# A two-layer encoder trunk: layer 1's modulation computed in the up passes, and no dots in its output projection

## The chip, the cores and the metric

The kernel runs on one core of a Trainium2 chip. The metric is the device time of one execution in microseconds. Matmuls run on TensorE (PE; its weight loads are PEld), elementwise work on VectorE (DVE), ScalarE (ACT) and GpSimd (POOL). All loads and stores are issued by SyncE (SP), whose queue is worked off in order: an issue that has to wait holds those behind it.

## The reference

The sequence has 1024 tokens of width 1024 in float32. Layer 0 mixes with multi-head latent attention, layer 1 with an mLSTM, and each is followed by a gated MLP with a causal convolution over three tokens. What matters here is the modulation: six vectors per layer, each 1024 long, computed from the conditioning vector c.

```python
c_act = jax.nn.silu(c)
for i in range(DEPTH):
    mod = c_act @ mod_w[i] + mod_b[i]
    sh_a, sc_a, g_a, sh_f, sc_f, g_f = [t[:, None, :] for t in jnp.split(mod, 6, axis=-1)]
    h = rms_norm(x) * (1 + sc_a) + sh_a
    y = mixer(h, ...)                      # layer 0: attention, layer 1: mLSTM; ends in @ w_out
    x = x + g_a * y
    h = rms_norm(x) * (1 + sc_f) + sh_f
    x = x + g_f * conv_ffn(h, ...)         # (gelu(conv(h @ w_up_a)) * (h @ w_up_g)) @ w_down
```

Parts 0 to 5 of a layer's modulation are, in this order, shift, scale and gate of the mixer and shift, scale and gate of the MLP.

## The kernel before

The activations lie with the channels on the partitions, as eight tiles of 128 channels by 512 tokens for each half of the sequence (`hf` 0 and 1). Every float32 product is made of three matmuls (`mm3`, L173 to L179), from operands split into a high and a low part. For a weight tile `wraw` or `raw`, ScalarE writes the high part `whi` (L169, L964) and GpSimd or VectorE the low part `wlo` (L170, L965).

A **dot** (`mod_dot`, L201) computes 128 entries of the modulation: a tile `mraw` of 128 rows of `mod_w` by 1024, 512 KB, is loaded (L213), VectorE multiplies it by the row `crow` = silu(c) and sums along the row into a column of `modc`. Eight dots make a part, and `mod_bias` (L206) adds the bias to it. `mod_steps` (L208) is a generator that deals this out: at each step it does the dot whose load was issued a step before, and then issues the next load. Its tiles have two buffers, so a load waits for the dot two before it. Dots are kept in the written order among themselves; everything else is ordered on each engine by the framework's scheduler from the order and the priority in which it is written.

The stages that the change touches are these.

- **Layer 0's MLP, up pass** (`mlp`, L941 on). 154 products of 12 matmuls, `pa`, `pb` and `pd`, numbered i = 0 to 153, with their operands derived by VectorE from `raw` tiles of `in_wf` (four buffers), then convolution (`ct`, L1004 to L1007) and gating (L1011), and a store of each result to memory (`ud`). After product i the function `extra(i)` is called; here it takes one step of layer 1's modulation at every third product from i = 30 on (L1275). Parts 1, 0 and 2 of layer 1, 24 dots, end about product 102.
- **Layer 0's down pass**, in the same sequence: its operands `U` are derived on VectorE from the stored values (`q`), its products `da` and `db` are gated into x (`gate_x`, L299).
- **Layer 1's mixer**, which uses `crow` as scratch; it is loaded and passed through silu again at L1626.
- **Layer 1's output projection** (`out_proj`, L848). For each half and each of the eight channel tiles m: load and split a weight tile (`unit`, L166 to L170), make the product `op` of 24 matmuls, gate it into x (L299), store x (`xd`, L846), square it on ScalarE (`sq`) and add the squares on VectorE (`ssq`, L246). The second half loads all eight weight tiles once more. After the first half, the sixteen small matmuls `st` (L255) sum the squares over the partitions, GpSimd takes the root (L260), and the transposes `rb` (L267) spread it; then x becomes the operands of the up pass. `up_ps` banks and `X_WAIT`, `X_RSTD` say how many products later this is written. Ahead of each m the projection calls `extra(hf, m)`: two steps of layer 1's modulation in the first half, one in the second (L1628 to L1630). These are parts 4 and 3, sixteen dots.
- **Layer 1's up pass**, which takes part 5, eight dots, from product 60 on, and its down pass with the final norm.

Of the kernel before, what the change touches and what calls it, by code (L numbers as in the profile page):

```python
# [11 lines left out]
F32 = mybir.dt.float32  # L12
# [6 lines left out]
P = 128  # L19
D = 1024  # L20
S = 1024
KT = D // P
HS = 512
# [64 lines left out]
U_MQ, U_MK, U_MV, U_MO, U_MG, U_OUT1 = 0, 4, 8, 16, 24, 25  # L88
# [11 lines left out]
def trunk_kernel(ctx: ExitStack, tc: tile.TileContext, xT, pos, c_d, cols_d, mod_w, win, winT, w0, w1, wf, wd, out):  # L100
# [4 lines left out]
    def nm(s):  # L105
        n_names[0] += 1
        return f"{s}_{n_names[0]}"
# [8 lines left out]
    def phase(name, **kw):  # L116
        st = ExitStack()
        p = st.enter_context(tc.tile_pool(name=name, bufs=1, reuse_waits="tile", **kw))
        return st, p
# [11 lines left out]
    def block(i, shape, dt, name):  # L131
        return blk.tile(shape, dt, tag=f"b{i}", name=nm(name))
# [67 lines left out]
    def mod_dot(l, i, raw):  # L200
        return dve.scalar_tensor_tensor(raw, raw, 1.0, crow, ALU.mult, ALU.mult, accum_out=modc[l][:, i:i + 1])  # L201

    def mod_bias(l, i, n=1):

        mc, b = modc[l][:, i:i + n], COL[f"mb{l}"] + i
        dve.scalar_tensor_tensor(mc, mc, 1.0 if i // 8 in (1, 4) else 0.0, cols_at(b, n), ALU.add, ALU.add)  # L206

    def mod_steps(l, parts, raw_tile, stop=None):  # L208

        for j in parts:  # L210
            for k in range(KT):
                raw = raw_tile()
                nc.sync.dma_start(raw, mod_w[l, j * 8 + k])  # L213
                yield
                tc.keep_in_program_order(mod_dot(l, j * 8 + k, raw))
            mod_bias(l, j * 8, KT)
            if j == stop:
                yield
# [100 lines left out]
    xs = [block(0, [P, KT, HS], F32, "x"), None]  # L319
# [437 lines left out]
    mods = mod_steps(0, (2, 4, 3, 5), lambda: mod_raw(), 3)  # L757
# [22 lines left out]
    def piece(gen, n=1):  # L780
        for _ in range(n):
            next(gen, None)
# [16 lines left out]
    for n in range(2 * NH):  # L799
        q, kk, qr, kvu, i, hf, head = args.pop(0)  # L800
# [47 lines left out]
    def out_proj(px, psC, osrc, us, w, l, extra=None, early=0):  # L848

        def up_ps(name):  # L850
            return psC.tile([P, HS], F32, tag="up", bufs=4, name=nm(name))

        stN, pn = phase("pn", side="right")
        xs, T = [], {}
        for hf in range(2):
            o, x = osrc(hf)
            xs.append(x)
            ssq = Squares(pn)
            for m in range(KT):
                if extra is not None:  # L860
                    extra(hf, m)
                if hf or m >= early:
                    ps = op_mm(o, us.pop(0) if us else unit(w[m]))
                    gate_x(x[:, m, :], m, ps, l, 2)
                store_x(2 * l, hf, m, x)
                ssq.keep(x[:, m, :]) if m == KT - 1 else ssq.add(x[:, m, :])
            if hf == 0:
                hh, hl = h_tiles(0)
                T["B11"], T["B21"] = [(hh[:, i:i + 4], hl[:, i:i + 4]) for i in (0, 4)]
                rstd_later(ssq, D, T["B11"], lambda rb: operands_first(xs[0], rb, l, hh, hl), X_WAIT[0],  # L870
                           up_ps, X_RSTD[0])
        for n, i in (("T1", 1), ("B22", 6), ("T2", 5), ("T3", 7)):
            t = (px if i > 5 else blk).tile([P, KT, HS], F32R, tag=f"b{i}", name=nm(n))
            T[n] = t[:, 0:4], t[:, 4:8]
        rstd_later(ssq, D, T["T1"], lambda rb: operands_second(px, xs, rb, l, T), X_WAIT[1], up_ps,
                   X_RSTD[1])
        stN.close()
        return xs, T
# [367 lines left out]
    pF = []  # L1246
# [3 lines left out]
    u_d = [[[dram.tile([P, HS], F32, name=f"ud{l}_{m}_{hf}") for hf in range(2)] for m in range(FT)] for l in range(2)]  # L1250

    stX, px, stP, psC = open_ffn(1)

    def o_src(hf):
        return (whole(o_back(1)), load_res(1, lambda hf, m: xT[m, :, hf * HS:(hf + 1) * HS])) if hf else oA

    stR, pr = phase("pr", side="right")
    mod_raw = lambda: pr.tile([P, D], F32, tag="mraw", bufs=2, name=nm("mraw"))
    xs, T = out_proj(px, psC, o_src, us, [w0[U_OUT0 + m] for m in range(KT)], 0,
                     lambda hf, m: piece(mods, MODS_OUT[hf][m]), EARLY)  # L1260
    for _ in mods:
        pass
    stR.close()
    mods = mod_steps(1, (1, 0, 2), lambda: pF[0].tile([P, D], F32, tag="mraw", bufs=2, name=nm("mraw")))
    hs = []

    def done(hf, t0, w, x, ssq):
# [4 lines left out]
                 W0[hf], W0_RSTD[hf])  # L1272

    pD = []
    mlp(px, psC, T, 0, u_d[0], pD, done, ((0, HS),), lambda i: piece(mods, i >= 30 and i % 3 == 0))  # L1275
    for _ in mods:
        pass
    h = hs
# [341 lines left out]
    stX, px, stP, psC = open_ffn(2)  # L1620

    def y_split(hf):
        return whole(split_o(hf, ys[hf])), load_res(hf, lambda hf, m: x_d[1][hf][m])

    stR, pr = phase("pr", side="right")
    nc.sync.dma_start(crow, c_d.broadcast_to([P, D]))  # L1626
    act.activation(crow, crow, AF.Silu)
    mods = mod_steps(1, (4, 3), lambda: pr.tile([P, D], F32, tag="mraw", bufs=2, name=nm("mraw")))  # L1628
    xs, T = out_proj(px, psC, y_split, [], [w1[U_OUT1 + m] for m in range(KT)], 1,
                     lambda hf, m: piece(mods, 2 if hf == 0 else 1))  # L1630
    for _ in mods:
        pass
    stR.close()
    mods = mod_steps(1, (5,), lambda: pF[0].tile([P, D], F32, tag="mraw", bufs=2, name=nm("mraw")))

    def gain(x, m):
# [14 lines left out]
    pD = []  # L1651
# [102 lines left out]
```

## Time and profile before

| what | value |
|---|---|
| three timed runs | 2292.92, 2294.84, 2308.62 us |
| median of the three | 2294.84 us |
| the profiled execution | 2296.64 us |
| span of its instructions | 2294.6 us |
| mean granted TensorE clock | 0.978 |

The span runs from the first to the last instruction; the 2.0 us by which the time is longer lie outside it. In a row of the timeline stand start, duration, engine, line, operation, what is written and what is read, and in brackets how long the engine was idle just before, with what ended that idle time. A row of a stretch has the busy time and the count of instructions for each engine, the clock that TensorE was granted as a share of its full speed, the mean busy share of the sixteen DMA engines and the rate. Matmuls overlap: one of 512 columns shows about 0.39 us, but starts follow each other by 0.227, so times of the stages are taken from starts.

Layer 0's up pass runs from 506.6 us to about 948, layer 1's output projection from 1519.0 to 1632.8, its up pass from there on.

### The profile page before, as it was taken

What the parts mean: (1) busy time and instruction counts of PE and PEld (TensorE: products, weight loads), DVE (VectorE), ACT (ScalarE), POOL (GpSimd) and SP (SyncE); (2) the same over time, 40 slices, a digit from 0 to 9 for tenths busy, and PEclk for the clock granted to TensorE, in tenths of its full rate; (3) what the DMA queues carried; (4) which work ended last, traced back from release to release, by engine and by line L of the source; (5) the groups of instructions that cost most, each with busy time, mean ns of one, the idle gap of its engine ahead of it and who ended that gap; (6) DMA issues with size and microseconds to landing.
All of it is one profiled execution on the core that took longest, in us unless ns stands there. A gap on an engine that the chain in (4) does not pass through costs nothing. (4 is left out here: it accounts for less than half of the span.)

```text
span 2294.6 us, 28893 instructions
## 1 busy us (share of the span) xinstructions
PE 2199.4 (96%) x10553; PEld 1838.3 (80%) x10553; DVE 1684.0 (73%) x2460; ACT 1037.9 (45%) x1810; POOL 691.8 (30%) x526
## 2 busy tenths in 40 slices
PE   8999999999999999999999899996999999999997
PEld 6778888887788888778878888975878888877786
DVE  7776777679888876899863524375696677679986
ACT  5365555446444444443434424343454444453335
POOL 3221112240343333342232222222313333333222
PEclk9989999999999999999999999997999999999999
DMA  8412334752444422543123111147232332245122
GB/s 292 144 47 61 97 106 134 262 188 80 140 158 145 144 76 90 184 147 111 60 79 86 57 37 46 56 158 244 99 132 88 102 120 92 83 146 208 51 83 74
DMA packets 104973, 269.98 MB, mean 118 GB/s; under 512 B 12352, under 2 KB 16000, under 8 KB 104832
## 3 DMA queue, kind: packets, MB, share of 16 engines
q1 hardware_dynamic: 104832, 268.15, 35.6%
q8 instruction: 83, 1.36, 0.2%
q14 instruction: 58, 0.48, 0.1%
HBM read 221.01 MB, written 44.47 MB: 116 GB/s over the span
## 5 line engine op out<-in xcount | busy, mean ns | idle before, releaser
L965 POOL TENSOR_TENSOR wlo<-raw,whi 128x512 fp32r<-128x512 f32 (+1 forms) x220 | 327.4, 1497 | 582.7 <-ACT whi L964 562.5
L170 POOL TENSOR_TENSOR wlo<-wraw,whi 128x1024 fp32r<-128x1024 f32 x64 | 157.3, 2462 | 298.2 <-ACT whi L169 248.1
L964 ACT ACTIVATE whi<-raw 128x512 fp32r<-128x512 f32 (+1 forms) x252 | 146.6, 605 | 221.2 <-PE pb L178 52.0
L177 PE MATMUL pa<-T,whi 128*128 128x512 f32 x528 | 208.1, 394 | 11.8 <-DVE g L1052 6.7
L179 PE MATMUL pa<-T,wlo 128*128 128x512 f32 x528 | 207.0, 392 | 1.9 <-DVE wlo L965 1.9
L178 PE MATMUL pa<-T,whi 128*128 128x512 f32 x528 | 206.6, 391 | 0.0
L964 ACT ACTIVATE whi<-wsum 128x512 fp32r<-128x512 f32 (+1 forms) x224 | 134.4, 616 | 140.9 <-PE pa L178 48.6
L965 POOL TENSOR_TENSOR wlo<-wsum,whi 128x512 fp32r<-128x512 f32 x72 | 102.3, 1420 | 178.4 <-ACT whi L964 178.3
L177 PE MATMUL da<-U,whi 128*128 128x512 f32 (+1 forms) x364 | 139.9, 384 | 3.2 <-DVE x L299 3.2
L178 PE MATMUL da<-U,whi 128*128 128x512 f32 (+1 forms) x364 | 139.2, 383 | 0.0
L179 PE MATMUL da<-U,wlo 128*128 128x512 f32 (+1 forms) x364 | 138.5, 382 | 0.0
L177 PEld LDWEIGHTS pa<-T,whi 128*128 128x128 f32 x528 | 99.8, 189 | 37.7 <-DVE g L1052 4.2
L1004 ACT ACTIVATE ct<-a,cols 128x512 f32<-128x512 f32 x88 | 71.1, 810 | 129.0 <-DVE a L1026 74.1
L965 DVE TENSOR_TENSOR wlo<-wsum,whi 128x512 fp32r<-128x512 f32 (+1 forms) x152 | 113.3, 754 | 20.0 <-ACT whi L964 19.3
L179 PEld LDWEIGHTS pa<-T,wlo 128*128 128x128 f32 x528 | 99.8, 189 | 23.7 <-DVE wlo L965 2.8
L169 ACT ACTIVATE whi<-wraw 128x1024 fp32r<-128x1024 f32 x67 | 70.8, 1058 | 105.6 <-PE inp L178 34.4
L178 PEld LDWEIGHTS pa<-T,whi 128*128 128x128 f32 x528 | 99.9, 189 | 20.4
L1118 DVE TENSOR_TENSOR U<-q,U 128x1024 fp32r<-128x1024 f32 x84 | 106.1, 1281 | 7.3 <-ACT U L1117 6.6
L177 PE MATMUL op<-oh,whi 128*128 128x512 f32 x256 | 100.8, 395 | 6.2 <-ACT whi L169 6.2
L178 PE MATMUL inp<-h,whi 128*128 128x512 f32 x256 | 103.5, 404 | 3.2 <-DVE h L283 3.2
L1007 ACT ACTIVATE ct<-ct 128x512 f32<-128x512 f32 x88 | 55.2, 630 | 113.0 <-DVE ct L1006 113.0
L179 PE MATMUL db<-U,wlo 128*128 128x512 f32 x264 | 102.6, 390 | 1.7 <-DVE wlo L965 1.7
(367 smaller groups left out, 6406.4 us busy)
## 6 DMA issues: line engine op xcount, KB each, us to landing
raw<-in_wf SPq DMA_DIRECT2D x96, 512.0 KB, 3.8
wraw<-in_w SPq DMA_DIRECT2D x67, 512.0 KB, 3.7
mraw<-in_mod_w SPq DMA_DIRECT2D x56, 512.0 KB, 4.2
ud<-ct SPq DMA_DIRECT2D x88, 256.0 KB, 2.9
q<-ud SPq DMA_DIRECT2D x88, 256.0 KB, 4.3
raw<-in_wd SPq DMA_DIRECT2D x32, 512.0 KB, 6.3
pa<-in_mod_w SPq DMA_DIRECT2D x24, 512.0 KB, 3.9
xd<-x SPq DMA_DIRECT2D x48, 256.0 KB, 2.9
```

Source lines behind the costliest of these rows:

```text
L169: act.activation(hi, raw, AF.Copy)
L170: (lo_eng or pool).tensor_tensor(lo, raw, hi.bitcast(F32), ALU.subtract)
L177: pe.matmul(ps, lh, rh, start=first, stop=False, skip_group_check=more)
L178: pe.matmul(ps[:, 0:rl.shape[-1]], lh, rl, start=False, stop=False, skip_group_check=more)
L179: pe.matmul(ps, ll, rh, start=False, stop=last, skip_group_check=more)
L964: act.activation(hi, src, AF.Copy)
L965: eng.tensor_tensor(lo, src, hi.bitcast(F32), ALU.subtract)
L1004: act.activation(t, a[:, 2:], AF.Identity, bias=col(f"cb{l}", m), scale=cw(m, 2))
L1007: act.activation(t, t, AF.Gelu)
L1118: dve.tensor_tensor(lo, w, hi.bitcast(F32), ALU.subtract)
```

## The change

Parts 4 and 3 of layer 1, sixteen dots with their loads and biases, leave layer 1's output projection and are appended to the three parts in layer 0's up pass, which then has 40 dots. The condition i >= 28 starts at the same product as i >= 30, since 30 is the first multiple of three in either case; so the first 24 dots stay where they are, the sixteen new ones belong to products 102 to 150, and no step is left when the pass ends. The pool `pr` of layer 1's projection, which held the two tiles for these dots, goes too. Part 5 stays in layer 1's up pass, and so the loading of `crow` stays. `out_proj` is then called without `extra`.

```diff
-    mods = mod_steps(1, (1, 0, 2), lambda: pF[0].tile([P, D], F32, tag="mraw", bufs=2, name=nm("mraw")))
+    mods = mod_steps(1, (1, 0, 2, 4, 3), lambda: pF[0].tile([P, D], F32, tag="mraw", bufs=2, name=nm("mraw")))
...
-    mlp(px, psC, T, 0, u_d[0], pD, done, ((0, HS),), lambda i: piece(mods, i >= 30 and i % 3 == 0))
+    mlp(px, psC, T, 0, u_d[0], pD, done, ((0, HS),), lambda i: piece(mods, i >= 28 and i % 3 == 0))
...
-    stR, pr = phase("pr", side="right")
     nc.sync.dma_start(crow, c_d.broadcast_to([P, D]))
     act.activation(crow, crow, AF.Silu)
-    mods = mod_steps(1, (4, 3), lambda: pr.tile([P, D], F32, tag="mraw", bufs=2, name=nm("mraw")))
-    xs, T = out_proj(px, psC, y_split, [], [w1[U_OUT1 + m] for m in range(KT)], 1,
-                     lambda hf, m: piece(mods, 2 if hf == 0 else 1))
-    for _ in mods:
-        pass
-    stR.close()
+    xs, T = out_proj(px, psC, y_split, [], [w1[U_OUT1 + m] for m in range(KT)], 1)
     mods = mod_steps(1, (5,), lambda: pF[0].tile([P, D], F32, tag="mraw", bufs=2, name=nm("mraw")))
```

The scheduler deals the instructions out anew. Before, SyncE's queue in layer 1's projection had this at the end of the first half (`xd_0_6` and `xd_0_7` are its last two stores, the x loads are the second half's, the two `wraw` its first weights):

```order
L846 DMA xd_0_6_4304<-x_13121 128x512
L213 DMA mraw_13385<-in_mod_w 128x1024
L732 DMA x_13484<-xd_1_3_4293 128x512
L213 DMA mraw_13424<-in_mod_w 128x1024
L732 DMA x_13484<-xd_1_4_4294 128x512
L213 DMA mraw_13427<-in_mod_w 128x1024
L846 DMA xd_0_7_4305<-x_13121 128x512
L732 DMA x_13484<-xd_1_5_4295 128x512
L732 DMA x_13484<-xd_1_6_4296 128x512
L732 DMA x_13484<-xd_1_7_4297 128x512
L166 DMA wraw_13496<-in_w 128x1024
L166 DMA wraw_13530<-in_w 128x1024
```

Now the same two weights (`wraw_13493` and `wraw_13527`) are found here, in the middle of the first half:

```order
L846 DMA xd_0_2_4300<-x_13168 128x512
L732 DMA x_13483<-xd_1_4_4294 128x512
L732 DMA x_13483<-xd_1_5_4295 128x512
L732 DMA x_13483<-xd_1_6_4296 128x512
L732 DMA x_13483<-xd_1_7_4297 128x512
L166 DMA wraw_13493<-in_w 128x1024
L846 DMA xd_0_3_4301<-x_13168 128x512
L166 DMA wraw_13527<-in_w 128x1024
L953 DMA raw_13832<-in_wf 128x1024
```

The first of them stood behind the first half's last store, and stands behind its third.

On TensorE the first half's statistics moved too. Before, they and the transposes stood between the halves; the end of them and the start of the second half were

```order
L255 MATMUL st_13549<-ones,ssq_13130 128x1
L255 MATMUL st_13549<-ones,sq_13462 128x1
L267 MATMUL rb_13598<-ident,rstd_13559 128x128 x4
L177 MATMUL op_13502<-oh_13466,whi_13498 128x512
L178 MATMUL op_13502<-ol_13467,whi_13498 128x512
```

Now they stand inside the second half's second product, 36 matmuls after the half's start:

```order
L177 MATMUL op_13533<-oh_13465,whi_13529 128x512
L178 MATMUL op_13533<-ol_13466,whi_13529 128x512
L179 MATMUL op_13533<-oh_13465,wlo_13530 128x512
L255 MATMUL st_13546<-ones,ssq_13177 128x1
L255 MATMUL st_13546<-ones,sq_13461 128x1
```

The transposes follow another 24 matmuls on, inside the third product, so two products and a half of the second half now run ahead of what needs the root.

The third place is VectorE at the turn from layer 0's up pass to its down pass. Before, the rows shortly ahead of the turn were

```order
L1006 SCALAR_TENSOR_TENSOR ct_8133<-a_8110,cols_4405,ct_8133 128x512
L1118 TENSOR_TENSOR U_8159<-q_8160,U_8159 128x1024 x2
L1052 TENSOR_TENSOR g_1337_8014<-g_1337_8014,pa_8020 128x512
L1011 TENSOR_TENSOR ct_8133<-ct_8133,g_1337_8014 128x512
L1026 TENSOR_TENSOR a_8184<-a_8184,pb_8209 128x512
```

and now there are two dots among them:

```order
L1006 SCALAR_TENSOR_TENSOR ct_8175<-a_8152,cols_4405,ct_8175 128x512
L201 SCALAR_TENSOR_TENSOR mraw_8117,modc_80<-mraw_8117,crow 128x1024
L1118 TENSOR_TENSOR U_8204<-q_8205,U_8204 128x1024 x2
L1052 TENSOR_TENSOR g_1349_8050<-g_1349_8050,pa_8059 128x512
L1011 TENSOR_TENSOR ct_8175<-ct_8175,g_1349_8050 128x512
L201 SCALAR_TENSOR_TENSOR mraw_8181,modc_80<-mraw_8181,crow 128x1024
L1026 TENSOR_TENSOR a_8229<-a_8229,pb_8257 128x512
```

The rows at the first gated sum of the down pass (L299) were

```order
L1052 TENSOR_TENSOR g_1356_8157<-g_1356_8157,pa_8171 128x512
L1118 TENSOR_TENSOR U_8271<-q_8160,U_8271 128x1024
L299 SCALAR_TENSOR_TENSOR x_8340<-da_8382,modc_79,x_8340 128x512
L1006 SCALAR_TENSOR_TENSOR ct_8307<-a_8268,cols_4405,ct_8307 128x512
L1118 TENSOR_TENSOR U_8312<-q_8272,U_8312 128x1024 x2
```

and are now, with the last dot and the bias of part 3 among them,

```order
L1052 TENSOR_TENSOR g_1371_8202<-g_1371_8202,pa_8216 128x512
L1118 TENSOR_TENSOR U_8319<-q_8205,U_8319 128x1024
L299 SCALAR_TENSOR_TENSOR x_8390<-da_8432,modc_79,x_8390 128x512
L201 SCALAR_TENSOR_TENSOR mraw_8253,modc_80<-mraw_8253,crow 128x1024
L1006 SCALAR_TENSOR_TENSOR ct_8357<-a_8316,cols_4405,ct_8357 128x512
L206 SCALAR_TENSOR_TENSOR modc_80<-modc_80,cols 128x8
L1118 TENSOR_TENSOR U_8362<-q_8320,U_8362 128x1024 x2
```

Three dots thus stand among the last up products' work, the last of them behind the first gated sum of the down pass.

## The prediction

> **What bounds the kernel now.** I read the page first, then the busy time of each engine in stretches of ten microseconds (to find where TensorE is not busy), then the timeline of TensorE inside the emptiest stretch, and last who issued what on VectorE and SyncE there. The page says that TensorE is the bound:
>
> ```profile
> PE 2199.4 (96%) x10553; PEld 1838.3 (80%) x10553; DVE 1684.0 (73%) x2460; ACT 1037.9 (45%) x1810; POOL 691.8 (30%) x526
> ```
>
> So a change pays only where TensorE stands still or runs at half clock. The largest such place is the middle of layer 1's output projection (columns: stretch, length, busy us and instructions of PE, PEld, DVE, ACT, POOL, granted clock, DMA share, GB/s):
>
> ```profile
> 1560.00:1570.00 10.00, 3.38 (x15) 2.51 (x13) 5.74 (x11) 0.63 (x1) 0.00 (x0) 0.88 0.74 248
> 1570.00:1580.00 10.00, 4.26 (x18) 3.78 (x18) 3.89 (x7) 0.63 (x1) 1.01 (x1) 0.50 0.96 325
> 1580.00:1590.00 10.00, 3.26 (x7) 2.15 (x8) 7.78 (x8) 6.99 (x9) 4.45 (x2) 0.50 0.45 159
> ```
>
> Three stretches with TensorE a third busy, the DMA engines nearly full, and the clock down to half. TensorE's timeline shows both halves of the projection, `op` being its products, `st` and `rb` the statistics of the first half, `pa` the first product of the up pass:
>
> ```profile
> 1519.00 0.49 PE L177 MATMUL op<-oh,whi 128*128 128x512 f32 x1
> ...
> 1562.44 0.39 PE L179 MATMUL op<-oh,wlo 128*128 128x512 f32 x1
> 1567.67 0.55 PE L255 MATMUL st<-ones,ssq 128*128 128x1 f32 x2 [4.85 <-DVE ssq L246]
> 1573.76 0.59 PE L255 MATMUL st<-ones,sq 128*128 128x1 f32 x2 [5.53 <-ACT sq L234]
> ...
> 1578.25 1.12 PE L267 MATMUL rb<-ident,rstd 128*128 128x128 f32 x4 [1.34 <-POOL rstd L260]
> 1585.53 0.80 PE L177 MATMUL op<-oh,whi 128*128 128x512 f32 x1 [6.16 <-ACT whi L169]
> ...
> 1632.80 0.39 PE L177 MATMUL pa<-h,whi 128*128 128x512 f32 x1
> ```
>
> Four waits in a row: on the sum of squares, on the last square, on its root, and on weights. What is late behind them is the dots. VectorE and SyncE at the end of the first half:
>
> ```profile
> 1571.09 1.22 DVE L201 SCALAR_TENSOR_TENSOR mraw<-mraw,crow 128x1024 f32<-128x1024 f32 x1 [1.48 <-DMA mraw<-in_mod_w]
> 1572.24 0.08 DVE L201 DVE_READ_ACCUMULATOR mraw<-mraw,crow 128x1 f32 x1
> 1572.24 0.74 DVE L299 SCALAR_TENSOR_TENSOR x<-op,modc,x 128x512 f32<-128x512 f32 x1
> ```
>
> ```profile
> 1573.01 0.32 SPq L846 DMA_DIRECT2D xd<-x  x1
> 1573.38 1.44 SPq L732 DMA_DIRECT2D x<-xd  x3
> 1574.91 0.92 SPq L166 DMA_DIRECT2D wraw<-in_w  x2
> ```
>
> The gated sum (L299) of a product that TensorE ended near 1562.7 runs at 1572.24, because dots in front of it wait one after another for their 512 KB; and the first weights of the second half leave SyncE at 1574.91, because stores of such late sums and loads of dots stand before them.
>
> **The change, part by part.** Term 1, the dots taken out of layer 1's projection. The first half's 192 products take 1562.44 + 0.23 − 1519.00 = 43.7 us, 0.227 each. The second half would need the same plus its own statistics, and it needs 1632.80 − 1562.67 = 70.1. How long statistics take at full clock is read where the second half's pass through TensorE:
>
> ```profile
> 1638.93 0.28 PE L255 MATMUL st<-ones,ssq 128*128 128x1 f32 x2
> ...
> 1640.63 0.48 PE L177 MATMUL pa<-h,whi 128*128 128x512 f32 x1
> ...
> 1643.48 0.60 PE L267 MATMUL rb<-ident,rstd 128*128 128x128 f32 x4
> ```
>
> That is 1.7 us, and about 0.4 more for `rb` (an estimate: four small matmuls, less than the 0.60 shown): 43.7 + 2.1 = 45.8, so 24.3 us are lost, waits and half clock together. Does all of it go? In the new order the statistics stand 36 products (8.2 us) behind the first half and the transposes 24 more, so VectorE, freed of these sixteen dots, has ended the sum when TensorE arrives:
>
> ```profile
> L201 DVE SCALAR_TENSOR_TENSOR mraw<-mraw,crow 128x1024 f32<-128x1024 f32 x16 | 22.9, 1433 | 13.2 <-DMA mraw<-in_mod_w 13.2
> ```
>
> 36 us of VectorE go (22.9 busy, 13.2 waiting). The first weights of the second half stand behind the third store of the first half. That store follows the third product, whose end is 1519.0 + 3 × 5.5, near 1535.5; with the four loads between, the weights leave near 1540 instead of 1574.91 and are wanted at 1562.7. They have some 20 us to spare, so I take the whole 24.3; the other bound, if only the wait for `whi` stayed, is 24.3 less 6.2 for the wait and about as much again for the half clock behind it (an estimate), about 12. One `raw` load now stands ahead of the first half's eight loads of x; the first load of a dot stood there before, of the same 512 KB, so that costs nothing.
>
> Term 2, sixteen dots and sixteen 512 KB loads added to the last third of layer 0's up pass. That pass has 24 dots now, up to 808 us, and none after; rows for the part with dots, without dots, and the turn to the down pass, and then the dot itself:
>
> ```profile
> 600.00:810.00 210.00, 207.89 (x915) 171.24 (x915) 169.16 (x224) 90.52 (x155) 80.85 (x66) 1.00 0.44 144
> 810.00:920.00 110.00, 110.00 (x487) 91.13 (x486) 75.88 (x92) 46.77 (x80) 41.56 (x36) 1.00 0.27 84
> 920.00:1000.00 80.00, 77.48 (x337) 62.07 (x335) 71.75 (x85) 36.46 (x53) 26.93 (x16) 1.00 0.55 186
> ```
>
> ```profile
> L201 DVE SCALAR_TENSOR_TENSOR mraw<-mraw,crow x24: 1210/1217/2305, 609.3 to 807.3; 128x1024 f32<-128x1024 f32 x24
> ```
>
> Sixteen dots of 1.3 us (1.22 and 0.08 for reading the sum) are 20.8 us; VectorE is idle for 110 − 75.9 = 34.1 us between 810 and 920, so most of it is hidden. The 24 dots cost TensorE at most 210 − 207.9 = 2.1 us; 16/24 of that is 1.4. The loads stand on SyncE between weights and stores, each behind the dot two before it. With DMA at 0.27 there is room, and 24 such loads cost no more than those 2.1 us. Bounds 0 and 3; I take 1.4.
>
> The Trainium skill ("SBUF — State Buffer", Who interferes with whom) says that a VectorE instruction with two SBUF inputs, which a dot is, and a GpSimd instruction that reads SBUF block each other entirely. By that, with GpSimd busy 42 of 110 us, sixteen dots would meet one 6 times and cost some 4 us more if nothing hid them (an estimate by that page): 2279.7 in place of the sum below. The longest of the 24 dots (2305 ns against 1217) fits the rule, the median says that it seldom happens.
>
> Term 3, the last three of these dots, which fall into the turn to the down pass. VectorE there:
>
> ```profile
> 923.67 2.36 DVE L1118 TENSOR_TENSOR U<-q,U 128x1024 fp32r<-128x1024 f32 x2 [2.01 <-ACT U L1117]
> ...
> 929.43 0.69 DVE L1026 TENSOR_TENSOR a<-a,pb 128x512 f32<-128x512 f32 x1 [1.38 <-PE pb L179]
> ...
> 946.07 0.74 DVE L299 SCALAR_TENSOR_TENSOR x<-da,modc,x 128x512 f32<-128x512 f32 x1
> ```
>
> The first two land ahead of the rows at 923.67 and 929.43, in gaps of 2.01 and 1.38 us, and cost nothing; without that cover 1.3 each. The third lands behind 946.07, where VectorE has no gap: 1.3, and the bias that follows it 0.1. Queued behind it are the conv, the splits of `U` and the next gated sums, which free TensorE's banks. I take 1.4; bounds 0 and 4.1. The down pass is also dealt out a little differently by the scheduler; I price that at 0, with 2 us either way.
>
> Term 4, the entry into layer 1's up pass, 24 us earlier and without the stall that let loads run ahead. The nearest rows are the first 90 us of the up pass in layer 0, where no stall precedes it, and in layer 1, with the longest wait of TensorE in the former:
>
> ```profile
> 506.60:596.60 90.00, 83.77 (x355) 67.26 (x354) 78.68 (x109) 50.45 (x77) 9.93 (x12) 0.94 0.31 104
> 1632.80:1722.80 90.00, 86.02 (x386) 70.22 (x385) 80.96 (x111) 53.18 (x81) 14.11 (x14) 1.00 0.34 117
> ```
>
> ```profile
> PE pa L177 <- DVE a L1045: 2.0, 1, 2.0
> ```
>
> Layer 0 starts 31 matmuls fewer (7.0 us), at a clock of 0.94. Bounds 0 and 7.0; I take 1.5, nearer to layer 1's own row. The Trainium skill ("TensorE: Matmul & The Clock Gate", The HAM clock gate) has the clock drop to half after an idle window of about 3.4 us. By that rule the entry, with waits under that, could not lose clock. The row of layer 0 disagrees: 0.94 with no wait above 2.0; by the rule the term would be near 0 and the sum 2274.2.
>
> **The sum.** −24.3 + 1.4 + 1.4 + 1.5 = −20.0. The profiled execution took 2296.64 us (span 2294.6 and 2.0 around it), which gives 2276.6. The median of the three runs shown, 2294.84, lies 1.8 lower and would give 2274.8. I start from halfway, 2295.7, here and in the rivals: **2275.7**.
>
> **The rivals.** (a) All added work is hidden. For it: layer 1's own up pass carries eight dots, and TensorE was busy throughout:
>
> ```profile
> 1820.00:1940.00 120.00, 120.00 (x531) 99.41 (x530) 92.68 (x119) 51.97 (x90) 45.25 (x37) 1.00 0.34 110
> ```
>
> Against: those are half as dense, and VectorE is full at 946. Terms 2 to 4 fall to 0, and the time is 2295.7 − 24.3 = 2271.4. (b) The weights of the second half stay late, since their tiles still wait for products four back: the wait for `whi` and part of the half clock stay, 12 us of term 1 remain, less 4.3: 2288.0. Against: the load of weights leaves 34 us earlier. (c) Layer 1's entry slips as layer 0's does: 7.0 for 1.5, so 2281.2. For it is that the two stages are now alike; against, that layer 0 loads its `o` from memory there. (d) The stall only moves. In the projection sixteen dots cost 24.3 us, 1.5 each, through SyncE: a load of a dot waits for a dot, and weights wait behind it. If SyncE is held likewise in layer 0's up pass, TensorE pays 24.3 there and 4.1 at the turn: 2295.7 − 24.3 + 28.4 = 2299.8, slower. It decides from the point at which a hold of SyncE outlasts the lead of the weights, which `raw` has four buffers for; against it are the 24 dots that cost 2.1 us in the same queue.
>
> **How the numbers follow.** Forecast 0.50, (a) 0.27, (b) 0.08, (c) 0.10, (d) 0.05. From (a) less the 2 us by which the lowest of the three runs lies under their median, to just short of (b), leaving out (b), (d) and some of the scatter: 2269 to 2287. One per cent, about what a measurement of this kernel can tell from no change, is 22.9 us: below 2271.9 lie two thirds of (a), which is close to that line, and a fifth of the forecast, together 0.28; a loss of over 1% would need (d) at several times its price, 0.02; within 1% lies the rest, 0.70.
>
> **What would show it.** Right: between the first `op` and the first `pa` of layer 1 some 89.5 us in place of 113.8, no wait of `st`, `rb` or `op` above 1.5 us, granted clock 1.00 through the stage; between 810 and 920 TensorE busy for 108 us or more, with VectorE near 97; one new wait of 1 to 2 us near 946. Wrong: `op` waiting for `whi` at the second half's start (b); a clock below 1.00 in the first 90 us of layer 1's up pass (c); SyncE's `raw` loads of layer 0 waiting for L201 and TensorE waiting for `whi` or `wlo` there (d).

## The result, and the profile after

| | runs | median us | lowest to highest |
|---|---|---|---|
| before | 8 | 2293.88 | 2287.93 to 2308.62 |
| changed | 8 | 2274.26 | 2272.09 to 2282.89 |

The ratio is 0.9911, with a 95% interval of 0.9886 to 0.9935: a gain of 0.65 to 1.14%, 19.6 us between the medians. The prediction had 2275.7. The profiled execution of the changed kernel took 2272.45 us, with a span of 2270.5.

The stretches of ten microseconds in the middle of layer 1's projection, changed kernel, where TensorE had been busy a third of the time at down to half clock (columns as before: busy us of PE, PEld, DVE, ACT, POOL, clock, DMA share, GB/s):

```profile
1510.00:1520.00 10.00, 10.00 (x37) 8.20 (x37) 8.61 (x14) 6.28 (x11) 0.23 (x1) 0.74 0.75 264
...
1550.00:1560.00 10.00, 10.00 (x46) 8.29 (x45) 3.89 (x3) 3.31 (x4) 4.55 (x2) 1.00 0.45 160
1560.00:1570.00 10.00, 10.00 (x54) 8.54 (x53) 1.31 (x3) 2.17 (x3) 3.62 (x3) 1.00 0.39 131
1570.00:1580.00 10.00, 10.00 (x48) 8.26 (x47) 9.06 (x8) 6.41 (x9) 2.39 (x1) 1.00 0.29 107
```

From 1520 on TensorE is busy throughout at full clock. One thing is new: a clock of 0.74 at the projection's start. TensorE's timeline of the changed kernel:

```profile
1505.33 1.03 PE L1476 MATMUL yT<-ident,ob 128*128 128x128 f32 x8
...
1509.15 2.27 PE L1476 MATMUL yT<-ident,ob 128*128 128x128 f32 x7 [1.97 <-DVE ob L1468]
1511.07 0.78 PE L177 MATMUL op<-oh,whi 128*128 128x512 f32 x1
...
1515.06 0.51 PE L177 MATMUL op<-oh,whi 128*128 128x512 f32 x1
...
1564.85 0.28 PE L255 MATMUL st<-ones,ssq 128*128 128x1 f32 x2
...
1572.12 0.60 PE L267 MATMUL rb<-ident,rstd 128*128 128x128 f32 x4
...
1602.53 0.39 PE L177 MATMUL pa<-h,whi 128*128 128x512 f32 x1
```

From the first `op` to the first `pa` it is 1602.53 − 1511.07 = 91.5 us, where it was 113.8. `st` and `rb` wait for nothing, nor does any `op`. The first nine matmuls took 3.99 us instead of nine times 0.227, so 1.95 of the 91.5 are half clock at the start. SyncE's queue shows the first weights of the second half, which had left at 1574.91:

```profile
1530.83 2.44 SPq L732 DMA_DIRECT2D x<-xd  x4
1533.49 0.45 SPq L166 DMA_DIRECT2D wraw<-in_w  x1
```

The second half begins 36 matmuls (the prediction calls them products), 8.2 us, ahead of `st`, near 1556.7, so the weights leave 23 us before they are wanted. In layer 0 the stretches that answer to 810 to 920 and 920 to 1000 (this execution was 6 to 7 us ahead there) and the first 90 us of layer 1's up pass read:

```profile
803.00:913.00 110.00, 109.83 (x485) 90.66 (x484) 92.16 (x119) 46.22 (x80) 44.25 (x36) 1.00 0.45 148
913.00:993.00 80.00, 75.25 (x328) 60.72 (x327) 76.23 (x90) 35.24 (x51) 25.52 (x14) 1.00 0.52 178
...
1602.50:1692.50 90.00, 84.97 (x374) 69.11 (x373) 80.20 (x110) 52.58 (x80) 13.78 (x13) 0.98 0.33 111
```

The first row holds thirteen of the sixteen dots, at almost no cost to TensorE (VectorE has 92 us there, where 97 had been announced: that sum had all sixteen in it), the second a loss at the turn: 75.3 busy of 80 where it had been 77.5. VectorE, GpSimd and TensorE of the changed kernel at the turn:

```profile
940.01 0.74 DVE L299 SCALAR_TENSOR_TENSOR x<-da,modc,x 128x512 f32<-128x512 f32 x1
940.67 1.21 DVE L201 SCALAR_TENSOR_TENSOR mraw<-mraw,crow 128x1024 f32<-128x1024 f32 x1
941.81 0.74 DVE L1006 SCALAR_TENSOR_TENSOR ct<-a,cols,ct 128x512 f32<-128x512 f32 x1
942.48 0.15 DVE L206 SCALAR_TENSOR_TENSOR modc<-modc,cols 128x8 f32<-128x8 f32 x1
942.55 3.44 DVE L1118 TENSOR_TENSOR U<-q,U 128x1024 fp32r<-128x1024 f32 x2
945.92 0.74 DVE L299 SCALAR_TENSOR_TENSOR x<-da,modc,x 128x512 f32<-128x512 f32 x1
946.58 1.11 DVE L1011 TENSOR_TENSOR ct<-ct,g 128x512 f32<-128x512 f32 x1
947.62 0.68 DVE L1011 TENSOR_TENSOR ct<-ct,pa 128x512 f32<-128x512 f32 x1
```

```profile
942.62 4.53 POOL L965 TENSOR_TENSOR wlo<-raw,whi 128x512 fp32r<-128x512 f32 x2 [6.48 <-ACT whi L964]
```

```profile
948.44 0.47 PE L177 MATMUL da<-U,whi 128*128 128x512 f32 x1 [1.19 <-DVE ct L1011]
```

In the kernel before, the same stretch of VectorE has

```profile
946.07 0.74 DVE L299 SCALAR_TENSOR_TENSOR x<-da,modc,x 128x512 f32<-128x512 f32 x1
...
947.39 2.35 DVE L1118 TENSOR_TENSOR U<-q,U 128x1024 fp32r<-128x1024 f32 x2
949.66 0.68 DVE L1011 TENSOR_TENSOR ct<-ct,g 128x512 f32<-128x512 f32 x1
```

The gating of `ct` (L1011) starts 6.57 us after the first gated sum where it had started 3.59 after it, 3.0 us later. The last dot and the bias make 1.2 of that. The two `U`, which take 3.44 us in place of 2.35 while GpSimd makes `wlo`, make 1.1, and a second gated sum (945.92), which the new order has ahead of `ct`, makes 0.7. TensorE waits 1.19 us for `ct`, 8 us behind that dot: the new wait that was announced near 946.

### The profile page after: what moved, and what is told of

Same layout as the page of the kernel before. It is cut to its first block, busy times and chain, and to the rows that moved or that the text cites. A ratio compares the mean times of both kernels' runs of the same rounds, so it can differ in the third digit from the quotient of the medians.

```text
span 2270.5 us, 28892 instructions
## 1 busy us (share of the span) xinstructions
PE 2189.2 (96%) x10553; PEld 1831.5 (81%) x10553; DVE 1686.1 (74%) x2460; ACT 1036.8 (46%) x1810; POOL 702.3 (31%) x526
## 4 chain that ended last, share of the span: by engine, by line
PE 36%; DVE 8%; DMA 2%; issue 2%; ACT 1%; POOL 1%; SPq 0%; DVEq 0%; POOLq 0%; ACTq 0%
PE pa L177 3%; PE pa L179 3%; PE pa L178 3%; PE inp L178 2%; PE inp L177 2%; PE inp L179 2%; PE pd L177 1%; PE pd L179 1%; PE pd L178 1%; PE op L177 1%; PE da L177 1%; PE da L179 1%; PE da L178 1%; PE op L178 1%; PE op L179 1%
## 5 line engine op out<-in xcount | busy, mean ns | idle before, releaser
L965 POOL TENSOR_TENSOR wlo<-raw,whi 128x512 fp32r<-128x512 f32 (+1 forms) x220 | 333.0, 1523 | 572.7 <-ACT whi L964 552.4
L965 POOL TENSOR_TENSOR wlo<-wsum,whi 128x512 fp32r<-128x512 f32 x72 | 107.7, 1496 | 174.1 <-ACT whi L964 173.9
L177 PE MATMUL db<-U,whi 128*128 128x512 f32 x264 | 103.3, 391 | 0.6 <-ACT whi L964 0.6
```

Source lines behind the costliest of these rows:

```text
L177: pe.matmul(ps, lh, rh, start=first, stop=False, skip_group_check=more)
L965: eng.tensor_tensor(lo, src, hi.bitcast(F32), ALU.subtract)
```

## The experiments

Twelve more runs were made, in three groups (e1 to e4, e5 to e8, f1 to f4; f1 is the changed kernel once more); each group has its own runs of the kernel before beside it (medians 2295.08, 2293.36 and 2295.90), and the ratio is to those. The stages are read from TensorE's timeline of each profiled execution: layer 0's up pass from the first `pa` on h to the last; turn and down pass from there to the transposes `rb` at its end; the projection from the first `op` to the first `pa`; layer 1's up pass like layer 0's.

| kernel | median us | ratio (95%) | up 0 | turn, down 0 | projection | up 1 |
|---|---|---|---|---|---|---|
| before | 2293.88 | | 416.87 | 227.83 | 113.80 | 407.07 |
| changed | 2274.26 | 0.9911 (0.9886–0.9935) | 413.90 | 230.42 | 91.46 | 409.69 |
| e1 left out | 2270.45 | 0.9893 (0.9873–0.9913) | 414.76 | 227.86 | 90.28 | 408.57 |
| e2 both | 2297.80 | 1.0016 (1.0000–1.0033) | 415.78 | 231.64 | 113.40 | 408.50 |
| e3 loads only | 2295.88 | 1.0005 (0.9990–1.0019) | 415.06 | 230.37 | 113.18 | 406.23 |
| e4 dots only | 2273.32 | 0.9923 (0.9895–0.9952) | 415.61 | 230.82 | 91.59 | 407.89 |
| e5 half loads | 2279.47 | 0.9934 (0.9921–0.9948) | 415.36 | 231.57 | 93.42 | 410.76 |
| e6 six buffers | 2289.27 | 0.9983 (0.9969–0.9997) | 414.27 | 230.11 | 106.81 | 411.42 |
| e7 both halves | 2273.90 | 0.9915 (0.9902–0.9928) | 415.07 | 230.61 | 91.49 | 408.10 |
| e8 earlier | 2273.30 | 0.9913 (0.9899–0.9927) | 418.68 | 227.91 | 91.08 | 407.11 |
| f1 changed again | 2271.53 | 0.9898 (0.9878–0.9917) | 414.34 | 230.69 | 91.62 | 407.32 |
| f2 part 3 in projection | 2277.20 | 0.9910 (0.9890–0.9930) | 415.52 | 227.83 | 93.15 | 411.40 |
| f3 from 18 | 2269.85 | 0.9887 (0.9870–0.9903) | 416.20 | 227.83 | 91.50 | 407.70 |
| f4 last four | 2271.03 | 0.9896 (0.9879–0.9912) | 415.88 | 228.29 | 91.56 | 407.58 |

**e1, the sixteen dots done nowhere.**

```diff
-    mods = mod_steps(1, (1, 0, 2, 4, 3), ...)
+    dve.memset(modc[1][:, 24:40], 0.0)
+    mods = mod_steps(1, (1, 0, 2), ...)
```

> The changed kernel without the sixteen dots of parts 4 and 3 in layer 0's up pass: they are done nowhere, so layer 1's scale and shift of the MLP are zero plus bias-free, and the rest is as it was. It gives term 1 by itself, and beside the changed kernel the price of terms 2 and 3. Theory (the sum on record: 24.3 us from the projection, 1.5 back at the entry into layer 1's up pass, 2.8 for the added dots): about 2271.5 us beside 2293.9 before and 2274.3 for the changed kernel, with the same 91 us between the first op and the first pa of layer 1. Rival 1, the added dots are wholly hidden: the same time as the changed kernel, 2274.3, within 1 us. Rival 2, the added dots cost more than the two new gaps show, since the lead of the changed kernel fell by 2.6 us from the turn to the end of layer 0's down pass and may have fallen elsewhere too: 2268 or less.

This kernel leaves the two vectors uncomputed. It took 2270.45 us. The turn is back at 227.86, the up pass as with the dots. So the added dots cost some 2.6 us in the trace, all of it at the turn; by the medians 1 to 4 (the changed kernel was timed at 2274.26 and, in f1, at 2271.53), which the scatter alone could make. Rival 1 falls by the trace.

**e2, the dots in both places.**

```diff
+    stR, pr = phase("pr", side="right")
...
+    mods = mod_steps(1, (4, 3), lambda: pr.tile([P, D], F32, tag="mraw", bufs=2, name=nm("mraw")))
-    xs, T = out_proj(px, psC, y_split, [], [w1[U_OUT1 + m] for m in range(KT)], 1)
+    xs, T = out_proj(px, psC, y_split, [], [w1[U_OUT1 + m] for m in range(KT)], 1,
+                     lambda hf, m: piece(mods, 2 if hf == 0 else 1))
```

> The sixteen dots are done twice: in layer 0's up pass as in the changed kernel, and again in layer 1's output projection as before. It gives terms 2 and 3 by themselves, on the kernel before. Theory: 2293.9 plus 2.8, so about 2296.7, with 113 us between the first op and the first pa of layer 1. Rival 1, added dots wholly hidden: 2293.9 within 1 us. Rival 2, the saving comes not from the dots leaving the projection but from something else that the new build of the rest brought (other half-clock windows): less than 2290, with 100 us or less in the projection.

2297.80, 0 to 0.33% over the kernel before, 113.4 us in the projection and 231.6 at the turn. Both the saving and the payment follow the dots with their loads; rival 2 falls.

**e3 and e4, what of a dot makes the stall.** In the changed kernel's projection e3 has the sixteen loads without dots, e4 the sixteen dots without loads, each two steps ahead of each channel tile of the first half as in e2.

```diff
+    def loads():
+        for j in (4, 3):
+            for k in range(KT):
+                raw = pr.tile([P, D], F32, tag="mraw", bufs=2, name=nm("mraw"))
+                nc.sync.dma_start(raw, mod_w[1, j * 8 + k])
+                yield
```

```diff
+        nc.sync.dma_start(raw, mod_w[1, 32])
+        yield
+        for j in range(2 * KT):
+            tc.keep_in_program_order(dve.scalar_tensor_tensor(
+                res, raw, 1.0, crow, ALU.mult, ALU.mult, accum_out=got[:, j:j + 1]))
+            yield
```

> The changed kernel, and in layer 1's output projection the sixteen loads of 512 KB as before, into tiles that nothing reads; no dots there. A load now waits only for the load two before it, not for a dot. The built order puts the first half's statistics between the halves again, as before the change. Theory (the stall came of the coupling: a load waits for a dot, stores and weights queue behind the load on SyncE, the dot waits for the load and holds the gated sums on VectorE): most of the stall stays away, at most a few us for eight MB more in a stage that moved 183 GB/s, about 2277 (2275 to 2282). Rival 1, the bytes alone make the weights late: the whole 22 us come back, 2294 to 2297. Rival 2, the order on TensorE makes the stall: with the statistics between the halves the root is exposed, some 6 us, 2280.

> The changed kernel, and in layer 1's output projection sixteen dots of the same shape on one resident tile, into columns that nothing reads: VectorE's work of before without its loads. The built order leaves TensorE's products and statistics as in the changed kernel. Theory (coupling): 20.8 us more on VectorE in a stage in which it was busy 51 of 91.5 us are mostly hidden; up to 2 us for gated sums that come 1.2 us later, 2274 to 2277. Rival, VectorE's time alone made the sums and so the statistics late: 10 us or more of the 22 come back, 2284 to 2296.

The theory of coupling failed in e3: loads that wait for no dot, with VectorE free of dots, bring the whole stall back, 113.18 us and 2295.88. What TensorE of e3 waited for in the projection (columns: who for whom, us in all, times, longest):

```profile
PE op L177 <- ACT whi L169: 11.7, 2, 8.5
PE op L179 <- POOL wlo L170: 2.4, 2, 1.2
PE st L255 <- ACT sq L234: 1.4, 1, 1.4
PE rb L267 <- POOL rstd L260: 1.3, 1, 1.3
```

It is weights: 14.1 of 16.8 us. The statistics, which e3's order has between the halves as before, wait 2.7, so rival 2 explains no more than that. And e4, with the same order as the changed kernel, has all of VectorE's dots and no stall:

```profile
L1633 DVE SCALAR_TENSOR_TENSOR mres<-mraw,crow x16: 1211/1214/1227, 1522.3 to 1563.5; 128x1024 f32<-128x1024 f32 x16
```

Sixteen dots within 41 us beside the gated sums, and the projection takes 91.59. So the loads bring the stall, and the arithmetic of the dots does not. What the loads do is seen from the DMA issues in the first half's 43.7 us. Kernel before, changed kernel, e3 (columns: count, KB each, median us from issue to landing):

```profile
mraw<-in_mod_w SPq DMA_DIRECT2D x11, 512.0 KB, 5.2
...
wraw<-in_w SPq DMA_DIRECT2D x2, 512.0 KB, 5.2
```

```profile
wraw<-in_w SPq DMA_DIRECT2D x6, 512.0 KB, 3.7
```

```profile
mraw<-in_mod_w SPq DMA_DIRECT2D x13, 512.0 KB, 4.9
...
wraw<-in_w SPq DMA_DIRECT2D x2, 512.0 KB, 6.4
```

Two of these weights are the first half's own last two in every kernel. The changed kernel issues four of the second half's besides, the kernel before and e3 none. And the same 43.7 us as one stretch, for the changed kernel, e3 and e7 (below) in turn:

```profile
1511.07:1554.77 43.70, 43.70 (x186) 36.02 (x185) 28.92 (x26) 15.90 (x23) 16.99 (x7) 0.95 0.76 267
```

```profile
1518.91:1562.61 43.70, 39.33 (x164) 31.61 (x163) 20.90 (x25) 12.73 (x19) 9.53 (x4) 0.92 0.88 292
```

```profile
1513.22:1556.92 43.70, 43.70 (x191) 36.12 (x190) 21.45 (x26) 14.04 (x21) 9.99 (x5) 0.98 0.88 305
```

The DMA engines are well used in this half in each of them, but a full DMA is not the difference: e7 has the share of e3, moves more, and does not stall. In e3 they even stand nearly still for 3 us shortly before the second half's weights leave, because SyncE's queue waits for a store, and the weights stand behind the last one:

```profile
1561.90:1564.90 3.00, 3.00 (x14) 2.47 (x14) 0.45 (x1) 0.00 (x0) 0.24 (x1) 1.00 0.03 11
```

```profile
1570.68 0.32 SPq L846 DMA_DIRECT2D xd<-x  x1
1571.04 2.36 SPq L732 DMA_DIRECT2D x<-xd  x5
1573.50 0.86 SPq L166 DMA_DIRECT2D wraw<-in_w  x2
```

The order of that queue is fixed when the program is built, and the scheduler dealt it out anew for each kernel.

**e5, e6, e7: bytes, or the hold of the queue.** All three are e3 with one thing changed: half the bytes of each load, six tiles for two, or one load ahead of each channel tile of both halves.

```diff
-                nc.sync.dma_start(raw, mod_w[1, j * 8 + k])
+                nc.sync.dma_start(raw[:, 0:HS], mod_w[1, j * 8 + k][:, 0:HS])
```

```diff
-                raw = pr.tile([P, D], F32, tag="mraw", bufs=2, name=nm("mraw"))
+                raw = pr.tile([P, D], F32, tag="mraw", bufs=6, name=nm("mraw"))
```

```diff
-                     lambda hf, m: piece(mods, 2 if hf == 0 else 1))
+                     lambda hf, m: piece(mods, 1))
```

> As the run with loads only (the changed kernel and sixteen loads into tiles that nothing reads, in layer 1's output projection), but each load takes the left half of the 128x1024 block: 256 KB, sixteen loads, 4.2 MB in place of 8.4. Loads alone had brought the whole stall back (113.2 us from first op to first pa, waits for whi of 3.15 and 8.52), so two theories are left. Bytes: the first half's 43.7 us hold 14.9 MB at the 340 GB/s that full stretches reached; half the bytes then fit, the stall goes nearly or wholly, 92 to 96 us in the stage and 2274 to 2279. Queue: each load holds SyncE until the load two before it has landed, and weights behind it wait; with as many loads as before at least half of the stall stays, 103 us or more and 2285 or more.

> As the run with loads only, 512 KB each, but with six tiles in place of two, so that a load waits for the load six before it and no longer holds SyncE for long. Bytes theory: the same 8.4 MB lie ahead of the second half's weights, the stall stays, 108 us or more in the stage, 2290 to 2298. Queue theory: the hold is gone, so most of the stall is, 95 to 100 us and 2276 to 2282.

> As the run with loads only, sixteen loads of 512 KB and two tiles, but one load ahead of each channel tile of both halves, in place of two ahead of each of the first half. The stage moves the same bytes. Bytes in the first half (theory): 4.2 MB fewer there, so little stall is left, 92 to 97 us in the stage, 2274 to 2279. Rival, bytes of the whole stage: 25 MB in 91.5 us, the stall stays wholly, 2294 to 2298. Queue theory: as many holds, spread, half of the stall or more, 2285 or more.

Half the bytes leave 2.0 of the 21.7 us; the same bytes spread over both halves leave nothing; six buffers leave 15. The stage came out as the bytes theory had it (e6 1 us under its mark of 108; of the times, e6 is 0.7 under its range and e5 0.5 over). The traces say less than that. In the first half's 43.7 us e3 moved 292 GB/s, e5 289, e6 312 and e7 305, so the two that do not stall carried about as many bytes there as the two that do. Nor do the holds stay as was assumed. What SyncE waited for loads in the first half of e3 and of e7:

```profile
SPq L1630 <- DMA mraw<-in_mod_w: 21.9, 11, 4.7
```

```profile
SPq L1630 <- DMA mraw<-in_mod_w: 1.3, 2, 1.1
```

In e6 none of the sixteen loads waits there for another, and 15 us of the stall remain: the hold by the buffers isn't needed for a stall. But e7, nearly free of holds too, doesn't decide between bytes and holds. What goes with the stall in all of these traces is what stands in SyncE's queue ahead of the second half's first weight (columns: how many of the first half's eight stores and how much of the dots' loads stand there, when the weight left after the first `op`, and the projection):

| kernel | stores ahead | loads ahead, MB | left, us | projection |
|---|---|---|---|---|
| before | 8 | 8.4 | 55.9 | 113.80 |
| e3 | 8 | 8.4 | 54.6 | 113.18 |
| e6 | 7 | 8.4 | 52.6 | 106.81 |
| e5 | 6 | 4.2 | 37.4 | 93.42 |
| e7 | 6 | 4.7 | 37.0 | 91.49 |
| f2 (below) | 6 | 4.2 | 37.1 | 93.15 |
| e4 | 3 | 0.5 | 23.3 | 91.59 |
| changed | 3 | 0 | 22.4 | 91.46 |

The first half's last two weights move likewise: in e6 they leave 36.3 and 37.8 us after the first `op`, in e3 27.7 and 34.0, in the changed kernel 11.4 and 16.6. e6's longest wait is 5.94 us for `whi` at 1557.19, at the start of the first half's seventh product: it is the first half's own weights that came late there. Loads ahead and stores ahead rise together in these kernels, since the scheduler moved the weights back behind both. So it is shown that the loads bring the stall, and that the weights stand behind them; whether the loads' bytes or the stores that the weights were put behind cost the time is not separated. Whether the sixteen loads could stay if the weights were issued ahead of them was not tried. e5 was slower in all than the projection says, by 3 us in the up pass of layer 1; so were e6 and f2, and why these three is not settled.

**e8, no dot left at the turn, by a denser end.**

```diff
-    ... lambda i: piece(mods, i >= 28 and i % 3 == 0))
+    ... lambda i: piece(mods, i >= 28 and i % (3 if i < 102 else 2) == 0))
```

> The changed kernel with its last sixteen dots in layer 0's up pass at every second product from 104 to 134 in place of every third from 105 to 150, so that VectorE has done all of them before the turn to the down pass. Theory (the added dots cost 3 to 4 us, as 2270.45 without them and 2297.8 against 2295.1 with them say, and that at the turn): the new gap of 1.35 us near 947 and the lost lead behind it go, 2271 to 2272.5. Rival: the dots cost in VectorE's time wherever they stand, or stand in the way of the denser stretch's weights: 2274 to 2277, with new gaps between 803 and 913.

Half right: the turn takes 227.91, but the up pass 418.68, some 4 us more than with one dot in three products, and the 2273.30 lie between the two forecasts. TensorE between 803 and 913 shows where (busy 106.76 for 109.83), and three waits there are for the gating's `g`, which VectorE makes:

```profile
803.00:913.00 110.00, 106.76 (x468) 87.20 (x467) 92.11 (x125) 45.14 (x77) 45.00 (x35) 1.00 0.44 146
```

```profile
PE pa L177 <- DVE g L1052: 3.1, 3, 1.4
```

**f1 to f4: the changed kernel again, and three versions without dots at the turn.** f2 takes part 3 to the projection, one dot for each tile of the first half; f3 starts the dots at product 18; f4 takes the last four dots to the projection.

```diff
-    mods = mod_steps(1, (1, 0, 2, 4, 3), ...)
+    mods = mod_steps(1, (1, 0, 2, 4), ...)
...
+    mods = mod_steps(1, (3,), ...)
+    xs, T = out_proj(..., 1, lambda hf, m: piece(mods, (2 if m == 0 else 1) if hf == 0 else 0))
```

```diff
-    ... lambda i: piece(mods, i >= 28 and i % 3 == 0))
+    ... lambda i: piece(mods, i >= 16 and i % 3 == 0))
```

```diff
+    JK = [(j, k) for j in (1, 0, 2, 4, 3) for k in range(KT)]
+    mods = mod_some(JK[:36], ...)
...
+    mods = mod_some(JK[36:], ...)
```

> The changed kernel once more, on the same chip as the three below, as their measure, and to see which stages repeat. Expected: 2274 (2272 to 2277); 91 to 92 us from first op to first pa, 230.4 to 231 from the last pa of h in layer 0's up pass to the rb at the end of its down pass (kernels with the sixteen dots at the turn took 230.1 to 231.6, those without 227.8 to 227.9). Where half-clock windows fall in the stages before 500 us and in the mixer may differ.

> Part 4 in layer 0's up pass, so that its dots end at product 126, and part 3, eight dots, in layer 1's output projection, one for each channel tile of the first half. Theory (it is the bytes of the loads ahead of the second half's weights that stall the projection: eight loads of 512 KB or sixteen of 256 KB in the first half cost 0 to 2 us there, sixteen of 512 KB cost 22): no stall, 91 to 94 us in the stage, and the turn free of dots, 228; 2271 to 2274. Rival, the dots' chain (a load waits for a dot, a gated sum waits behind it): half the dots, half the stall, 102 us, 2282 or more.

> The changed kernel with the dots of layer 0's up pass at every third product from 18 to 138 in place of 30 to 150: as dense as there, and none left at the turn. Theory (at one in three products they cost next to nothing, at one in two they cost 3.7 us, and at the turn 2.9): the turn takes 228 in place of 230.8, and 2271 to 2272 in all. Rival: the first products, where VectorE was busy 79 of 90 us, pay instead: an up pass longer by 3 us or more than the 415 of the changed kernel, 2274 to 2277.

> The changed kernel with 36 dots in layer 0's up pass, the last at product 138, and the last four of part 3 in the first half of layer 1's output projection (2.1 MB). Theory: no dot at the turn, 228 there; four loads in the projection cost nothing, 91 to 92; 2271 to 2272. Rival, dots in the projection cost 22/16 us each: 5.5 us, 97 us in the stage, 2276 to 2278.

f1 repeats the stages that the change touches (230.69 and 91.62), at a median a little below its expected range. In f2 eight whole dots in the projection cost 1.7 us there, not 11, and the weights stand there behind the sixth store; but its up pass in layer 1 took 411.40, and with 2277.20 it is above its forecast. f4 does as expected, and so does the turn of f3, 228. f3 does pay in its up pass, though less than the 3 us that its rival asked for: 416.20, where f1 took 414.34, and the waits of TensorE for the gating's `g` in that pass (f3, then f1) are

```profile
PE pa L177 <- DVE g L1052: 6.0, 6, 1.6
```

```profile
PE pa L177 <- DVE g L1052: 2.6, 3, 1.3
```

f3 is the fastest, 2269.85 against 2271.53 for the changed kernel beside it; the intervals overlap, so by the times alone it isn't shown to be better. By the trace it is 2.9 us shorter at the turn and 1.9 longer before it.

## Why the prediction was right, and where not

**The total** came out 1.4 us from the forecast. By the profiles the terms come to −22.3 + 2.9 and 0.3 to 2.6 for the fourth, −17 to −19 beside −20.0 forecast and −19.6 between the medians (−24.4 in the group of f1): the sizes hold within the scatter, and one cause was half wrong. That the total is so near is partly luck: the measured gain has an interval of 15 to 26 us, and terms 2 and 3 were each off and cancelled.

**Term 1** (−24.3): the projection went from 113.80 to 91.46, so 22.3 us. All four waits went, and the weights left 22.4 us after the first `op`, where 21 had been announced. The missing 2.0 us are the 1.95 of half clock at the start, without which it is the 89.5 that was named. Of the cause, one half failed: "because dots in front of it wait one after another for their 512 KB" described what VectorE showed, but e4 has those dots with no stall, and e3 has the stall without them. The waits of `st` for sums were where the lateness showed. The other half stands: the first weights of the second half left late, "because stores of such late sums and loads of dots stand before them", and e3, where the loads alone are back, has them behind the last store again. What the loads' bytes add to this the runs leave open. The prediction called the DMA engines nearly full in the three empty stretches and made no term of it; its rows say that of one of the three (0.74, 0.96, 0.45).

**Term 2** (+1.4): about nothing. The profiles with the sixteen dots at products 102 to 150 have 413.9 to 415.8 us for layer 0's up pass, the two without them 414.8 and 416.9. **Term 3** (+1.4) was too small: the turn and the down pass took 230.1 to 231.6 with three dots at the turn (eight profiles, mean 230.8) and 227.8 to 228.3 without (six, mean 227.9), so 2.9. Before and after, as one stretch each:

```profile
923.50:1151.33 227.83, 223.41 (x984) 182.30 (x983) 209.08 (x250) 93.35 (x145) 75.71 (x51) 1.00 0.37 125
```

```profile
917.20:1147.62 230.42, 223.18 (x985) 182.61 (x983) 213.26 (x255) 93.45 (x145) 82.11 (x52) 1.00 0.37 126
```

TensorE does the same work at full clock and stands idle 7.2 us where it was 4.4. The announced wait is 1.19 us of the difference; the rest comes in the down pass behind it, where TensorE waits longer for splits and gated sums. That part had been priced at 0, with 2 us either way. The announced wait is no fixed part of the price either: e2 and e5, where the two `U` behind the last dot take 2.34 and 2.35 us, don't have it; they lose some half clock in that stage (0.99) and take 231.6. Together the two terms were right, 2.9 for 2.8, by errors that cancel.

**Term 4** (+1.5): not to be told from scatter. The same program had 374 matmuls in the first 90 us of layer 1's up pass in one profile and 385 in f1:

```profile
1607.60:1697.60 90.00, 87.25 (x385) 71.08 (x384) 81.07 (x112) 53.28 (x82) 13.95 (x13) 0.98 0.34 117
```

The pass as a whole was 2.6 us longer than before in the one and 0.3 in the other.

**The rivals.** (a) falls by the turn. (b) and (d) did not happen; and (d)'s mechanism, a load that waits for a dot, is not needed for the stall in the projection, which e3 has without it. In layer 0 thirteen of the loads, 6.8 MB, took the DMA share from 0.27 to 0.45 over 110 us, and TensorE stayed busy for 109.83 of them. (c) shows its sign, a clock of 0.98 in the first 90 us of layer 1's up pass, in both profiles, but not its price: against 386 matmuls before, 12 are missing in the one, 2.7 us, and 1 in the other, not 7.0 us.

**Not of the change.** The two profiled executions differ by 24.1 us in span. The stages that it touches make 22.3 + 3.0 − 2.6 − 2.6 = 20.1, and the 3.0 of layer 0's up pass are less half clock (granted 0.99 before, 1.00 after), which the added dots don't explain. The other 4.0 lie in stages whose code is the same: 3.3 us ahead of that pass, 4.2 in the mixer (367.67 and 363.45 us, and 366.08 in f1), −3.5 behind layer 1's up pass, where the granted clock was 0.98 before and 0.96 after. A sum against a single profile would be off by that much.

## What to carry to other kernels

A wait names the operation that came last, not what made it late: before a stall is put down to the engine that shows it, run the stalled stage once with the loads alone and once with the arithmetic alone. Then read the DMA queue in its order: which loads stand ahead of the weights that came late, and which stores, that wait for results, stand ahead of them too. A high DMA share alone did not make a stall here. And side work on a nearly full VectorE is paid where VectorE has no room: the sixteen dots cost nothing that shows at one in three products late in the up pass, some 4 us at one in two, and the three at the turn between two passes 2.9 us.

## What the runs showed of the hardware

**The half clock at the projection's start.** Before the projection TensorE does only transposes for 5.7 us, with a longest wait of 1.97 us (the rows at 1505.33 and 1509.15). In the profile of the changed kernel and ten others the clock is halved there or within the first microsecond of the projection; in the kernel before, e2 and e3 it is not, though that wait is as long. The Trainium skill ("TensorE: Matmul & The Clock Gate", The HAM clock gate) says that activity is judged over a window of about 3.4 us that runs freely, so that the same program meets it at different phases. That fits f1 and the profile after, where the same code has other windows, and the rows here show that such a window need not be without matmuls; why just the three kernels with the whole stall are spared, no run here shows.

**VectorE and GpSimd.** The dots of e4 show the exclusion that the prediction weighed (the Trainium skill, "SBUF — State Buffer", Who interferes with whom). GpSimd's `wlo` and VectorE's dots of e4:

```profile
1525.50 3.17 POOL L170 TENSOR_TENSOR wlo<-wraw,whi 128x1024 fp32r<-128x1024 f32 x1 [10.34 <-ACT whi L169]
1530.94 2.40 POOL L170 TENSOR_TENSOR wlo<-wraw,whi 128x1024 fp32r<-128x1024 f32 x1 [2.27 <-ACT whi L169]
...
1563.58 3.45 POOL L170 TENSOR_TENSOR wlo<-wraw,whi 128x1024 fp32r<-128x1024 f32 x1 [3.04 <-ACT whi L169]
```

```profile
1525.21 1.21 DVE L1633 SCALAR_TENSOR_TENSOR mres<-mraw,crow 128x1024 f32<-128x1024 f32 x1
...
1563.54 1.22 DVE L1633 SCALAR_TENSOR_TENSOR mres<-mraw,crow 128x1024 f32<-128x1024 f32 x1
```

A `wlo` that starts while a dot runs is longer than 2.40 by about what is left of the dot: 0.77 for 0.92, 1.05 for 1.18. So the trace agrees with the rule; but it is GpSimd that waited here, which had the time, and the projection took 91.59 us with dots and 91.46 without. At the turn of the changed kernel it was VectorE that waited: of the two `U` at 942.55 the second took 2.31 us in place of 1.21, while GpSimd's `wlo`, begun at 942.62, ran.
